# First block of the input projection: row scaling in halves ahead of all lo parts, and the hi products of three column groups in a row

## The chip, the cores and the metric

The kernel runs on one core of one Trainium2 chip. The metric is the device time of one execution in microseconds (us). Before the change the median of three runs was 921.94 us (920.85 to 922.54); the execution that was profiled took 920.29 us.

The engines are called PE (matrix products and transposes), DVE (vector work, two inputs), ACT (scalar work with one input: casts, copies, squares, activations), POOL (small scalar chains and some DMA issues) and SP (issues most DMAs). Each works its own list of instructions in order and waits on semaphores for the others.

## The reference, cut to what matters

There are 2048 prompt rows and 32 sample rows of width 1024. They run through one layer and a final norm:

```
hn   = rmsnorm(h, g_mix)                       # x * rsqrt(mean(x^2) + eps) * g
proj = hn @ w_in                               # 1024 -> 3072, six groups of 512 columns
hA, bA, cA, zA, vB, zB = split(proj)
u = cA * hA ;  c = causal width-3 conv(u) + bias ;  yA = bA * c * silu(zA)
yB = ((trailing mean(vB) - vB) @ pool_w) * pool_scale * silu(zB)
h += concat(yA, yB) @ w_out
h += (p @ w_ple) * sigmoid(rmsnorm(h, g_ple) @ w_gate)
y  = rmsnorm(h, g_final)
```

Everything is float32. A large product of two float32 operands is made of three PE products of rounded parts: each operand is split into a hi part (the value rounded to the PE's short float32 form) and a lo part (value minus hi), and hi*hi, hi*lo and lo*hi are added in PSUM.

## The kernel before

**Tiling.** The 2080 rows are cut into five blocks of 416 rows (`NB`). Blocks 0 and 1 form the first group. For the first of four column slices (`j = 0`), the first group is worked by `Unit.plain`: for each of the six column groups, 24 products of 128x128 weights by 128x416 rows per block, 8 pieces of the 1024 inner dimension by three part pairs. All later units use a scheme with seven products in place of eight; they are not touched.

**How the first block comes in.** SP loads rows 0 to 383 as three tiles of 128 rows, and then a fourth tile of 64 rows (the last 32 rows of block 0 and the last 32 of block 1). For each tile:

- ACT squares the row and adds it up (L89, `ssq_x`), POOL makes 1/root of it in two instructions (L70 `ms_x`, L74 `rstd_x`),
- DVE scales the tile by `rstd_x` and the gain (L407, `normal`),
- PE transposes it, four 128-column pieces to a PSUM bank, so two banks a tile: `pt_0_0` is the first half of tile 0, `pt_0_1` the second half (L416, `turn`),
- ACT writes the hi part with a cast (L78), DVE the lo part with a subtraction (L79), both from PSUM into the block's operand `B` (in `put`, by `split`).

The raw weights `raw_firstzb`, `raw_firstv` and `raw_firstc` of the first three column groups are split into hi and lo in the same way, as `w_firstzb`, `w_firstv` and `w_firstc`, two halves each.

**What PE does then.** `project` (L581) sorts the first product, `zb`, by part pair: 8 products hi*hi, 8 with the lo part of the rows, 8 with the lo part of the weights. All others (L564, `half_product`) take the three pairs for each piece in turn. After `zb` and `v` of block 0 come the transposes of block 1 (`pt_3`, `pt_0`, `pt_1`), the first half of `c`, the transposes `pt_2`, the second half of `c`, and then `zb` of block 1.

**Banks.** Six PSUM banks (`ps_m`) hold the transposes and products of this stage. A new tile takes the bank that came free longest ago in the program; the instruction that first writes it waits for the last reader of the old one. In the built program, the banks of `pt_0_0` and `pt_0_1` of block 0 go to its `pt_3_0` and `pt_3_1`, that of `pt_1_0` to `zb`, that of `pt_1_1` to `v`. In block 1, `pt_1_0` takes the bank of `zb` and `pt_1_1` that of `v`.

**What sets the order.** A scheduler orders each engine's instructions from the code; `keep_in_program_order` pins those it is called on to the order in which they are written. `second_block` is a generator whose steps (statistics, transposes, sums of block 1) are called between the products of block 0.

Of the kernel before, what the change touches and what calls it, by code (L numbers as in the profile page):

```python
# [12 lines left out]
ALU = mybir.AluOpType  # L13
PSUM = bass.MemoryType.PSUM

P = 128
D = 1024
KC = D // P
# [17 lines left out]
def trunk(ctx, tc, x_p, x_s, c_conv, c_pool, p_p, p_s, g_mix, w_in, conv_w, conv_b, pool_w,  # L36
# [294 lines left out]
    with ExitStack() as s1:  # L331
# [17 lines left out]
        def put(piece, src):  # L349

            return split(piece[:, :, 0], piece[:, :, 1], src)
# [52 lines left out]

        def normal(x, later=False):
            xt, n, r = x
            ins = nc.vector.scalar_tensor_tensor(xt[:n], xt[:n], r[:n], g_bc[:n], op0=ALU.mult, op1=ALU.mult)  # L407
            if later:
                tc.keep_in_program_order(ins)
# [156 lines left out]

        begun = []

        def project(ps, w, tb, between=None):
            x = hn[tb]  # L570
            if begun:
                for half in range(2):
                    half_product(ps, w[half], x[half], half == 0, half == 1)
                    if between and not half:
                        between()
                return

            begun.append(tb)
            steps = sorted(((k, a, b) for k in range(KC) for a, b in ((0, 0), (0, 1), (1, 0))), key=lambda t: t[1:])
            for i, (k, a, b) in enumerate(steps):  # L580
                nc.tensor.matmul(ps[:, :NB], w[k // KH][:, k % KH, a], x[k // KH][:, k % KH, b], start=i == 0,  # L581
                                 stop=i == len(steps) - 1)

# [9 lines left out]
        short0 = x_tile("0_3", [x_rows(0, 3), x_rows(1, 3)])  # L593
        B0.update(six(0))
        for c, x in enumerate([*ahead0, short0]):
# [84 lines left out]
        class Unit:  # L680
# [994 lines left out]
```

## Time and profile before

| | |
|---|---|
| median of three runs | 921.94 us |
| the profiled execution | 920.29 us |
| its span, first to last instruction | 918.5 us |
| PE busy | 904.2 us, 98% of the span |
| DVE busy | 722.4 us, 79% |
| ACT busy | 478.3 us, 52% |
| POOL busy | 150.8 us, 16% |

The span begins with the first instruction and ends with the last; the execution's own time is 1.8 us longer. Busy shares are means over the whole span. Where the order of a stage is in question, the list of instructions in order of time for that stage is the view to read, since shares do not tell which wait ended last.

### The profile page before, as it was taken

To read this page: it belongs to the slowest core of one execution; us is meant where nothing else is said; L and a number is where in the kernel's file an instruction comes from. 1 tells how busy PE (TensorE), PEld (TensorE's weight loads), DVE (VectorE), ACT (ScalarE), POOL (GpSimd) and SP (SyncE) were. 2 spreads that over 40 slices of the span, in tenths; PEclk is the share of its full clock that TensorE was granted. 3 is DMA by queue.
4 is the path that set the end of the run, shared out by engine and by line. 5 is a ranking of instruction groups with operands and counts; after the bars stand their busy time and mean duration, and the time that the engine had idled before them with its cause. 6 is when DMAs were issued, how large, how long until landed. Compare 5 with 4: busy or idle time off the path is not lost.

```text
span 918.5 us, 12937 instructions
## 1 busy us (share of the span) xinstructions
PE 904.2 (98%) x4485; PEld 819.3 (89%) x4485; DVE 722.4 (79%) x1231; ACT 478.3 (52%) x883; POOL 150.8 (16%) x271
## 2 busy tenths in 40 slices
PE   7999999999999999999999999999999999999996
PEld 5999999999999999999999988888877868888885
DVE  6996989999488989785777679765554799888965
ACT  6744565554345555443545456334334786565555
POOL 4111322212001111000000011111111002233333
PEclk9999999999999999999999999999999999999998
DMA  8245695779935546357655359755785886799893
GB/s 267 80 151 150 163 270 161 201 206 314 415 113 164 184 157 191 110 177 274 200 172 168 130 186 303 260 191 177 247 229 158 290 262 167 187 230 241 210 258 103
DMA packets 140734, 186.37 MB, mean 203 GB/s; under 512 B 12060, under 2 KB 111260, under 8 KB 139389
## 3 DMA queue, kind: packets, MB, share of 16 engines
q1 hardware_dynamic: 120237, 126.33, 45.0%
q0 software_dynamic: 17696, 53.71, 20.1%
q10 hardware_dynamic: 2736, 5.51, 1.8%
q8 instruction: 35, 0.57, 0.3%
q14 instruction: 30, 0.25, 0.1%
HBM read 128.93 MB, written 56.56 MB: 202 GB/s over the span
## 4 chain that ended last, share of the span: by engine, by line
PE 97%; DVE 1%; issue 1%; ACT 0%; DMA 0%; POOL 0%; SPq 0%; ACTq 0%; DVEq 0%; POOLq 0%
PE x_o L168 9%; PE x_g L168 9%; PE x_zbv L564 7%; PE x_ch L564 7%; PE x_zab L564 7%; PE e L103 5%; PE z_g L168 5%; PE z_o L168 4%; PE z_zbv L564 3%; PE z_ch L564 3%; PE z_zab L564 3%; PE v L564 3%; PE c L564 3%; PE b L564 3%; PE za L564 3%; PE h L564 3%
## 5 line engine op out<-in xcount | busy, mean ns | idle before, releaser
L78 ACT CAST y_S<-y_fS 128x512 fp32r<-128x512 f32 x32 | 19.3, 622 | 38.6 <-PE x_o L168 19.0
L103 PE MATMUL e<-wq,pps 128*128 128x512 f32 (+1 forms) x156 | 38.9, 400 | 0.2 <-ACT pps L78 0.2
L168 PE MATMUL x_o<-wo_b,y_S 128*128 128x512 f32 x128 | 35.8, 391 | 0.0
L168 PE MATMUL x_g<-wg_b,g_S 128*128 128x512 f32 x128 | 35.7, 389 | 0.0
L564 PE MATMUL z_zbv<-B,w_zbv_S 128*128 128x416 f32 x168 | 34.2, 352 | 0.0
L564 PE MATMUL x_ch<-B,w_ch_S 128*128 128x416 f32 x168 | 34.1, 351 | 0.0
L564 PE MATMUL z_zab<-B,w_zab_S 128*128 128x416 f32 x168 | 34.1, 351 | 0.0
L564 PE MATMUL x_zab<-B,w_zab_S 128*128 128x416 f32 x168 | 34.0, 351 | 0.0
L564 PE MATMUL x_zbv<-B,w_zbv_S 128*128 128x416 f32 x168 | 34.0, 351 | 0.0
L564 PE MATMUL z_ch<-B,w_ch_S 128*128 128x416 f32 x168 | 34.0, 351 | 0.0
L103 PEld LDWEIGHTS e<-wq,pps 128*128 128x128 f32 (+1 forms) x156 | 27.4, 182 | 7.0 <-ACT pps L78 0.5
L1402 POOL DMA_DIRECT2D e<-h_d x28 | 24.8, 906 | 52.9 <-DVE e L1399 45.9
L564 PEld LDWEIGHTS x_zab<-B,w_zab_S 128*128 128x128 f32 x168 | 31.3, 188 | 0.4
L564 PEld LDWEIGHTS x_zbv<-B,w_zbv_S 128*128 128x128 f32 x168 | 31.4, 188 | 0.3
L564 PEld LDWEIGHTS z_ch<-B,w_ch_S 128*128 128x128 f32 x168 | 31.4, 188 | 0.3
L564 PEld LDWEIGHTS z_zab<-B,w_zab_S 128*128 128x128 f32 x168 | 31.3, 188 | 0.3
L564 PEld LDWEIGHTS x_ch<-B,w_ch_S 128*128 128x128 f32 x168 | 31.3, 188 | 0.3
L564 PEld LDWEIGHTS z_zbv<-B,w_zbv_S 128*128 128x128 f32 x168 | 31.3, 188 | 0.4
L70 POOL TENSOR_SCALAR ms_x<-ssq_x 128x1 f32<-128x1 f32 (+2 forms) x18 | 11.0, 610 | 123.2 <-ACT junk L89 118.7
L78 ACT CAST y<-y 128x512 fp32r<-128x512 f32 x24 | 14.8, 618 | 29.2 <-PE x_o L168 14.6
L78 ACT CAST g_S<-g_fS 128x512 fp32r<-128x512 f32 x32 | 19.0, 618 | 18.5 <-DVE g_fS L1578 11.9
L168 PEld LDWEIGHTS x_o<-wo_b,y_S 128*128 128x128 f32 x128 | 24.0, 188 | 5.1 <-ACT c_o L1205 0.3
(598 smaller groups left out, 2651.5 us busy)
## 6 DMA issues: line engine op xcount, KB each, us to landing
y<-y_d SPq DMA_DIRECT2D x16, 512.0 KB, 5.6
x<-in_x_prompt_dram SPq DMA_DIRECT2D x16, 512.0 KB, 5.6
h_d<-x SPq DMA_DIRECT2D x16, 512.0 KB, 2.6
hn<-h_d SPq DMA_DIRECT2D x61, 128.0 KB, 6.2
xt<-in_x_prompt_dram SPq DMA_DIRECT2D x15, 512.0 KB, 5.4
e<-e_d SPq DMA_DIRECT2D x15, 512.0 KB, 6.4
e<-h_d POOLq DMA_DIRECT2D x28, 256.0 KB, 6.5
out_dram<-e POOLq DMA_DIRECT2D x13, 512.0 KB, 4.2
```

Of the source, the lines that this page charges most:

```text
L70: nc.gpsimd.tensor_scalar(ms[:n], ssq[:n], scalar1=1.0 / D, scalar2=EPS, op0=ALU.mult, op1=ALU.add)
L78: ins = nc.scalar.copy(hi, src)
L103: nc.tensor.matmul(ps[:n], pps[:, a, k, :n], wp[k][b][:, cs], start=k + q == 0, stop=k == 1 and q == 2)
L168: nc.tensor.matmul(ps[:n], lhs[:, k, a, :n], w[b][:, k], start=start and k + q == 0, stop=k == KH - 1 and q == 2, skip_group_check=True)
L564: nc.tensor.matmul(ps[:, :NB], lhs[:, k, x], b[:, k, y], start=start and k + q == 0, stop=stop and k == KH - 1 and q == 2, skip_group_chec ...
L1402: nc.gpsimd.dma_start(ee, h_d[r:r + P, at[1] * NH:at[1] * NH + NH], accum_op=ALU.add)
```

## The change

Three things are rewritten, all of them for block 0 of the first group at `j = 0`:

- `normal` takes a slice of columns. The four tiles of block 0 are scaled in eight steps of half a row each, all of them pinned, before the transposes are written. The lo parts, which stood between the scalings, come behind them.
- The hi casts of block 0 are pinned to the order in which they are written. The squares of the fourth tile come out ahead of all of them.
- `upper_parts` starts `zb`, `v` and `c` with their hi*hi products (8 each) in three banks, before anything else of these three is done. `lower_parts` adds the rest: 8 with the lo part of the rows, then 8 with the lo part of the weights. For `c` the rest is done half by half, with the transposes of block 1 between. Products of block 0 in these three groups are pinned.

The number of products, casts and subtractions and the numbers that they compute stay the same; only the four scalings become eight.

```
-        def normal(x, later=False):
+        def normal(x, later=False, cs=slice(0, D)):
             xt, n, r = x
-            ins = nc.vector.scalar_tensor_tensor(xt[:n], xt[:n], r[:n], g_bc[:n], op0=ALU.mult, op1=ALU.mult)
+            ins = nc.vector.scalar_tensor_tensor(xt[:n, cs], xt[:n, cs], r[:n], g_bc[:n, cs], op0=ALU.mult,
+                                                 op1=ALU.mult)
...
+        def part_of(ps, w, tb, half, a, b, start=False, stop=False):
+
+            x = hn[tb]
+            for k in range(KH):
+                tc.keep_in_program_order(
+                    nc.tensor.matmul(ps[:, :NB], w[half][:, k, a], x[half][:, k, b], start=start and k == 0,
+                                     stop=stop and k == KH - 1, skip_group_check=True))
+
+        def upper_parts(kind, w, tb):
+
+            ps = bank(f"{kind}_first")
+            for half in range(2):
+                part_of(ps, w, tb, half, 0, 0, start=half == 0)
+            begun[kind] = ps
+
+        def lower_parts(ps, w, tb, between):
+
+            order = [(half, *p) for p in ((0, 1), (1, 0)) for half in range(2)]
+            if between:
+                order.sort()
+            for i, (half, a, b) in enumerate(order):
+                part_of(ps, w, tb, half, a, b, stop=i == 3)
+                if between and i == 1:
+                    between()
...
+        for x in (*ahead0, short0):
+            for half in range(2):
+                normal(x, True, slice(half * NH, half * NH + NH))
         for c, x in enumerate([*ahead0, short0]):
-            normal(x)
             n = P if c < 3 else DEC
             for half, q in enumerate(("11", "21")):
-                put(B0[q][:, :, :, c * P:c * P + n], turn(x, half, f"pt0_{c}_{half}", bank)[:, :, :n])
+                ins = put(B0[q][:, :, :, c * P:c * P + n], turn(x, half, f"pt0_{c}_{half}", bank, True)[:, :, :n])
+                tc.keep_in_program_order(ins)
...
                 def product_of(kind, b, w, between=None):
+                    if kind in begun:
+                        ps = begun.pop(kind)
+                        lower_parts(ps, w, tbs[b], between)
+                        return ps[:, :NB]
...
                     wc = weights("c", j, f"c{tag}")
+                    for kind, w in (("zb", wz), ("v", wv), ("c", wc)):
+                        upper_parts(kind, w, tbs[0])
```

**DVE, the first block.** In the rows, `xt` is a tile of input rows, `B` the block's operand, `pt_a_b` half b of tile a transposed; the last numbers only tell buffers apart. Before:

```order
L407 SCALAR_TENSOR_TENSOR xt_0_162<-xt_0_162,rstd_x_0_168,g_bc 128x1024
L407 SCALAR_TENSOR_TENSOR xt_1_170<-xt_1_170,rstd_x_1_176,g_bc 128x1024
L407 SCALAR_TENSOR_TENSOR xt_2_178<-xt_2_178,rstd_x_2_184,g_bc 128x1024
L79 TENSOR_TENSOR B_0_195<-pt_0_0_199,B_0_195 128x4x128
L79 TENSOR_TENSOR B_0_195<-pt_0_1_206,B_0_195 128x4x128
L407 SCALAR_TENSOR_TENSOR xt_3_186<-xt_3_186,rstd_x_3_193,g_bc 64x1024
L79 TENSOR_TENSOR B_0_195<-pt_1_0_214,B_0_195 128x4x128
L79 TENSOR_TENSOR B_0_195<-pt_1_1_221,B_0_195 128x4x128
```

And now:

```order
L407 SCALAR_TENSOR_TENSOR xt_0_162<-xt_0_162,rstd_x_0_168,g_bc 128x512 x2
L407 SCALAR_TENSOR_TENSOR xt_1_170<-xt_1_170,rstd_x_1_176,g_bc 128x512 x2
L407 SCALAR_TENSOR_TENSOR xt_2_178<-xt_2_178,rstd_x_2_184,g_bc 128x512 x2
L407 SCALAR_TENSOR_TENSOR xt_3_186<-xt_3_186,rstd_x_3_193,g_bc 64x512 x2
L79 TENSOR_TENSOR B_0_195<-pt_0_0_206,B_0_195 128x4x128
L79 TENSOR_TENSOR B_0_195<-pt_0_1_213,B_0_195 128x4x128
L79 TENSOR_TENSOR B_0_195<-pt_1_0_220,B_0_195 128x4x128
L79 TENSOR_TENSOR B_0_195<-pt_1_1_227,B_0_195 128x4x128
L79 TENSOR_TENSOR B_0_195<-pt_2_0_234,B_0_195 128x4x128
```

The two lo parts of tile 0 (`pt_0_0`, `pt_0_1`) stood ahead of the fourth tile's scaling and stand behind it now.

**ACT, the same stage**, before:

```order
L89 ACTIVATE raw_firstc,ssq_x_2_180<-xt_2_178 128x1024
L78 CAST B_0_195<-pt_0_0_199 128x4x128
L78 CAST B_0_195<-pt_0_1_206 128x4x128
L89 ACTIVATE junk,ssq_x_3_189<-xt_3_186 64x1024
L78 CAST B_0_195<-pt_1_0_214 128x4x128
L78 CAST B_0_195<-pt_1_1_221 128x4x128
L78 CAST B_0_195<-pt_2_0_229 128x4x128
L78 CAST B_0_195<-pt_2_1_236 128x4x128
L78 CAST w_firstzb_259<-raw_firstzb 128x4x128
L78 CAST B_0_195<-pt_3_0_244 128x4x32
L78 CAST B_0_195<-pt_3_1_251 128x4x32
L78 CAST w_firstzb_262<-raw_firstzb 128x4x128
```

And now:

```order
L89 ACTIVATE raw_firstc,ssq_x_2_180<-xt_2_178 128x1024
L89 ACTIVATE junk,ssq_x_3_189<-xt_3_186 64x1024
L78 CAST B_0_195<-pt_0_0_206 128x4x128
L78 CAST B_0_195<-pt_0_1_213 128x4x128
L78 CAST B_0_195<-pt_1_0_220 128x4x128
L78 CAST B_0_195<-pt_1_1_227 128x4x128
L78 CAST B_0_195<-pt_2_0_234 128x4x128
L78 CAST B_0_195<-pt_2_1_241 128x4x128
L78 CAST B_0_195<-pt_3_0_248 128x4x32
L78 CAST w_firstzb_263<-raw_firstzb 128x4x128
L78 CAST B_0_195<-pt_3_1_255 128x4x32
L78 CAST w_firstzb_266<-raw_firstzb 128x4x128
```

The fourth tile's squares moved ahead of the hi casts. The first weight cast (`w_firstzb`, first half) stood ahead of the cast of `pt_3_0` and stands behind it now.

**PE, the first products**, before:

```order
L416 MATMUL pt_3_0_244<-ident,xt_3_186 128x64 x4
L416 MATMUL pt_3_1_251<-ident,xt_3_186 128x64 x4
L581 MATMUL zb_0_0_325<-B_0_195,w_firstzb_259 128x416 x4
L581 MATMUL zb_0_0_325<-B_0_195,w_firstzb_262 128x416 x4
L564 MATMUL v_0_0_351<-B_0_195,w_firstv_266 128x416
L581 MATMUL zb_0_0_325<-B_0_195,w_firstzb_259 128x416 x4
L581 MATMUL zb_0_0_325<-B_0_195,w_firstzb_262 128x416 x4
L581 MATMUL zb_0_0_325<-B_0_195,w_firstzb_259 128x416 x4
L581 MATMUL zb_0_0_325<-B_0_195,w_firstzb_262 128x416 x4
L564 MATMUL v_0_0_351<-B_0_195,w_firstv_266 128x416 x11
L564 MATMUL v_0_0_351<-B_0_195,w_firstv_269 128x416 x12
```

And now:

```order
L417 MATMUL pt_3_1_255<-ident,xt_3_186 128x64 x4
L582 MATMUL zb_first<-B_0_195,w_firstzb_263 128x416 x4
L582 MATMUL zb_first<-B_0_195,w_firstzb_266 128x416 x4
L582 MATMUL v_first<-B_0_195,w_firstv_270 128x416 x4
L582 MATMUL v_first<-B_0_195,w_firstv_273 128x416 x4
L582 MATMUL c_first<-B_0_195,w_firstc_279 128x416 x4
L582 MATMUL c_first<-B_0_195,w_firstc_282 128x416 x4
L582 MATMUL zb_first<-B_0_195,w_firstzb_263 128x416 x4
L582 MATMUL zb_first<-B_0_195,w_firstzb_266 128x416 x4
L582 MATMUL zb_first<-B_0_195,w_firstzb_263 128x416 x4
L582 MATMUL zb_first<-B_0_195,w_firstzb_266 128x416 x4
L582 MATMUL v_first<-B_0_195,w_firstv_270 128x416 x4
```

All hi*hi products of `zb`, `v` and `c` stand first now, so 8 products of `c` are ahead of the rest of `zb` and `v`. In the built program the three started products hold three of the six banks at once, and the banks are handed out anew behind them: in block 1, `pt_1_0` takes the bank of `v`, and `pt_1_1` that of block 1's `pt_3_0`, whose last reader is ACT's copy of it into `xt_3`.

**ACT, behind the copy of `v`** (`V`), where block 1's transposes are read, before:

```order
L798 COPY V_0_321<-v_0_0_351 128x416
L78 CAST B_12_285<-pt_3_0_386 128x4x32
L78 CAST B_2_197<-pt_3_1_394 128x4x32
L78 CAST pw<-raw_pw 128x512
L78 CAST B_12_285<-pt_0_0_402 128x4x128
L627 COPY xt_3_186<-pt_3_0_386 128x128
```

And now:

```order
L823 COPY V_0_325<-v_first 128x416
L78 CAST B_12_289<-pt_3_0_399 128x4x32
L78 CAST B_2_197<-pt_3_1_407 128x4x32
L78 CAST B_12_289<-pt_0_0_415 128x4x128
L78 CAST B_2_197<-pt_0_1_423 128x4x128
L648 COPY xt_3_186<-pt_3_0_399 128x128
```

The cast of `pw` went ahead of the copy of `V`, and the cast of `pt_0_1` came ahead of the copy of `pt_3_0` into `xt_3`.

More of the change, by code (lines that the diff above doesn't have):

```diff
@@ L565, in half_product @@
                                      stop=stop and k == KH - 1 and q == 2, skip_group_check=True)
-        begun = []
+        begun = {}
         def project(ps, w, tb, between=None):
             x = hn[tb]
[L571 to L582, printed above, removed]
+            for half in range(2):
+                half_product(ps, w[half], x[half], half == 0, half == 1)
+                if between and not half:
+                    between()
[17 more added lines that the diff above has]
+                if between and i == 1:
+                    between()
         B0 = {}
@@ L594, in trunk @@
         B0.update(six(0))
+        for x in (*ahead0, short0):
+            for half in range(2):
+                normal(x, True, slice(half * NH, half * NH + NH))
         for c, x in enumerate([*ahead0, short0]):
-            normal(x)
             n = P if c < 3 else DEC
             for half, q in enumerate(("11", "21")):
-                put(B0[q][:, :, :, c * P:c * P + n], turn(x, half, f"pt0_{c}_{half}", bank)[:, :, :n])
+                ins = put(B0[q][:, :, :, c * P:c * P + n], turn(x, half, f"pt0_{c}_{half}", bank, True)[:, :, :n])
+                tc.keep_in_program_order(ins)
         hn[0] = B0["11"], B0["21"]
```

## The prediction

> **What bounds the kernel now.** I read the page of the profile first: busy shares, and the chain of work that ended last.
>
> ```profile
> span 918.5 us, 12937 instructions
> PE 904.2 (98%) x4485; PEld 819.3 (89%) x4485; DVE 722.4 (79%) x1231; ACT 478.3 (52%) x883; POOL 150.8 (16%) x271
> PE 97%; DVE 1%; issue 1%; ACT 0%; DMA 0%; POOL 0%; SPq 0%; ACTq 0%; DVEq 0%; POOLq 0%
> ```
>
> PE carries 97% of the chain. Next, the view of waits for PE (who was waited for, us in total, times, longest):
>
> ```profile
> PE gm L376 <- DMA gm_row<-in_g_mix_dram: 2.4, 1, 2.4
> PE pt L416 <- DVE xt L407: 2.3, 1, 2.3
> PE pt L416 <- issue: 1.3, 1, 1.3
> PE x_zab L564 <- DVE U L880: 0.3, 1, 0.3
> PE e L103 <- ACT pps L78: 0.2, 1, 0.2
> ```
>
> The first three lie in the first 15 us; behind them PE waits 0.5 us in 900. So whatever delays PE in the first 35 us stays in the time almost whole, and there is little for the change to win behind its own place. Third, PE's instructions in order of time (start, length, name, count):
>
> ```profile
> 8.44 4.87 PE L416 MATMUL pt<-ident,xt 128*128 128x128 f32 x24 [2.29 <-DVE xt L407]
> 14.61 0.68 PE L416 MATMUL pt<-ident,xt 64*128 64x64 f32 x8 [1.29 <-issue]
> 15.39 2.88 PE L581 MATMUL zb<-B,w_firstzb 128*128 128x416 f32 x8
> 18.07 0.55 PE L564 MATMUL v<-B,w_firstv 128*128 128x416 f32 x1
> 18.41 3.51 PE L581 MATMUL zb<-B,w_firstzb 128*128 128x416 f32 x16
> 21.77 4.50 PE L564 MATMUL v<-B,w_firstv 128*128 128x416 f32 x23
> 26.20 2.60 PE L416 MATMUL pt<-ident,xt 64*128 64x64 f32 x24
> 34.17 2.06 PE L564 MATMUL zb<-B,w_firstzb 128*128 128x416 f32 x10
> ```
>
> From 15.39 on every row begins where the one before lets it. The first nine products take (18.41 - 15.39)/9 = 0.34 us each, the 23 of `v` (26.20 - 21.77)/23 = 0.193. The view by windows tells why (length, PE busy, number, granted clock, DMA):
>
> ```profile
> 12.36:15.77 3.41, 2.01 (x18) 0.99 1.11 346
> 15.77:19.18 3.41, 3.41 (x12) 0.51 0.71 248
> 19.18:22.59 3.41, 3.41 (x20) 1.00 0.78 221
> ```
>
> In one stretch of 3.41 us the clock was half, behind a stretch in which PE was busy for 2.01 of 3.41 us.
>
> **Part 1: when the first product can start.** Here DVE, POOL and ACT set the time. DVE:
>
> ```profile
> 7.10 1.28 DVE L407 SCALAR_TENSOR_TENSOR xt<-xt,rstd_x,g_bc 128x1024 f32<-128x1024 f32 x1 [0.22 <-ACT raw_firstv L89]
> ...
> 10.83 1.28 DVE L407 SCALAR_TENSOR_TENSOR xt<-xt,rstd_x,g_bc 128x1024 f32<-128x1024 f32 x1 [0.72 <-POOL rstd_x L74]
> 12.04 1.28 DVE L79 TENSOR_TENSOR B<-pt,B 128x512 fp32r<-128x512 f32 x2
> 13.24 1.27 DVE L407 SCALAR_TENSOR_TENSOR xt<-xt,rstd_x,g_bc 64x1024 f32<-64x1024 f32 x1
> 14.43 2.86 DVE L79 TENSOR_TENSOR B<-pt,B 128x512 fp32r<-128x512 f32 x6
> 19.62 1.28 DVE L79 TENSOR_TENSOR w_firstc<-raw_firstc,w_firstc 128x512 fp32r<-128x512 f32 x2
> ```
>
> POOL (`ms_x` of tile 1, `rstd_x` of tiles 2 and 3, then block 1):
>
> ```profile
> 7.12 0.19 POOL L70 TENSOR_SCALAR ms_x<-ssq_x 128x1 f32<-128x1 f32 x1 [0.42 <-ACT raw_firstv L89]
> ...
> 10.25 0.55 POOL L74 TENSOR_TENSOR rstd_x<-ms_x,nhalf 128x1 f32<-128x1 f32 x1
> 12.43 0.54 POOL L74 TENSOR_TENSOR rstd_x<-ms_x,nhalf 64x1 f32<-64x1 f32 x1
> 19.32 1.63 POOL L70 TENSOR_SCALAR ms_x<-ssq_x 128x1 f32<-128x1 f32 x1 [6.35 <-ACT junk L89]
> 21.04 0.55 POOL L74 TENSOR_TENSOR rstd_x<-ms_x,nhalf 128x1 f32<-128x1 f32 x1
> 21.67 1.28 POOL L70 TENSOR_SCALAR ms_x<-ssq_x 128x1 f32<-128x1 f32 x1
> ```
>
> ACT:
>
> ```profile
> 9.08 0.19 ACT L89 ACTIVATION_READ_ACCUMULATOR raw_firstc<-xt 128x1 f32 x1
> 13.88 0.63 ACT L78 CAST w_firstzb<-raw_firstzb 128x512 fp32r<-128x512 f32 x1
> 15.07 0.52 ACT L78 CAST B<-pt 128x128 fp32r<-128x128 f32 x2 [0.56 <-PE pt L416]
> ```
>
> Before: the fourth scaling ends at 13.24 + 1.27 = 14.51, its transposes start at 14.61, their cast at 15.07, and the product at 15.39 as soon as the first of the two casts is done. `w_firstzb` had been cast at 13.88, in ACT's idle time.
>
> Now the squares of the fourth tile follow those of the third at 9.27 and end near 10.4 instead of 12.1. That gain is mostly lost on POOL. Its 0.2 us step `ms_x` took 1.63 us at 19.32 and ended at 20.95, just behind DVE's row that ends at 19.62 + 1.28 = 20.90: while DVE runs such rows back to back, POOL stands still, at the borders between them too. The row at 21.67, 0.05 us behind the start of a scaling, is the same again. So `ms_x` of tile 3 finds POOL free at 10.80, comes 0.05 us behind the third tile's scaling at 10.83, and gets through at its end: 10.83 + 1.28 + 0.05 = 12.16; 0.08 to the next as from 20.95 to 21.04, then 0.55 of `rstd_x`: 12.79. The scaling in two halves I take at 1.28 as the whole one was; if each half costs as a 512-wide row of 0.68, less the overlap of 0.08, it is the same. It ends at 14.07, 0.44 earlier than before.
>
> But the lo parts now stand behind it, and the transposes need the banks that these free: one row each 0.60 us, ends at 14.67, 15.27 and 15.87. `pt_3_0` starts at 14.72, `pt_3_1` at 15.33 (before: 14.61, and the last four right behind), and `zb` needs the third lo part's bank: 15.93. On ACT, the cast of `pt_3_0` runs from 15.17 and the cast of the first weights, now behind it, from 15.34 for 0.63: 15.97. Both ends agree: the first product starts at 16.0, **0.6 us later**. The nearest rows bound this: if POOL slips through ahead of the third scaling (as its row at 7.12 did, 0.02 us behind a start), all of it is 0.68 earlier and the start is the old one; if the weight cast waited for both small casts, it would be 0.2 more.
>
> What the later start costs depends on the clock: in the half-clock stretch a product takes 0.34 instead of 0.193, so a later start of 0.6 loses 0.6/0.34 = 1.8 products, worth 0.35 us at full speed, and a little more as the clock was still full up to 15.77. I take **+0.4**; with another position of the stretch it is up to +0.6.
>
> **Part 2: the products.** Their number is the same. 8 products of `c` (8 x 0.193 = 1.54 us) move ahead of the rest of `zb` and `v`. `zb` and `v` end 1.54 us later and `c` is shorter by the same behind them: nothing by itself. Its cover is the time between the end of `v` and block 1's `zb`, which falls from 34.17 - 26.20 = 7.97 to 6.43 us. What has to be done in it is on ACT and DVE:
>
> ```profile
> 26.30 0.51 ACT L798 COPY V<-v 128x416 f32<-128x416 f32 x1 [2.79 <-PE v L564]
> 26.71 0.50 ACT L78 CAST B<-pt 128x128 fp32r<-128x128 f32 x2
> 27.11 0.62 ACT L78 CAST pw<-raw_pw 128x512 fp32r<-128x512 f32 x1
> 27.62 0.59 ACT L78 CAST B<-pt 128x512 fp32r<-128x512 f32 x1
> 28.10 0.28 ACT L627 COPY xt<-pt 128x128 f32<-128x128 f32 x1
> 32.95 0.69 DVE L79 TENSOR_TENSOR B<-pt,B 128x512 fp32r<-128x512 f32 x1
> ```
>
> The last row is the lo part of `pt_2_0`, which block 1's `zb` needs with its second product: 33.64 against 34.36, a slack of 0.7. In the changed order the lo part of `pw` and that of `f` (0.60 us a row each) are no longer ahead of it, so it comes 7.44 - 1.2 = 6.2 us behind the end of `v`, against a need at 6.43 + 0.19 = 6.6: it still fits.
>
> **Part 3: a new wait.** `pt_1_1` of block 1 now writes the bank that ACT's copy of `pt_3_0` frees. Counted from the start of the transposes (26.20 before): the cast of `pt_0_0` can start when its four transposes are done, some 1.3 behind (8 small ones and 4 at 0.11, 0.27 for the last one's end, 0.1 at the start); at 27.62 it came at 1.42 with the cast of `pw` ahead. Then the cast of `pt_0_1` at 0.48 behind, then the copy, again 0.48 behind, for 0.28: it ends at 1.33 + 0.48 + 0.48 + 0.28 = 2.57. `pt_1_1` was issued 20 transposes behind the start, at 2.0. PE waits to 2.63: **+0.63**. Behind this wait stand on PE the rest of `c` and all that follows; DVE and ACT gain time by it, so the lo part above fits all the more. The ends: nothing, if the cast of `pt_0_1` were not in the way (-0.48) and the rows ran at their shortest; 0.8, if each of the four rows takes 0.04 more, as the cast of 0.63 at 13.88 did against that of 0.59.
>
> **What is hidden.** `zb`'s activation and the copy of `V` come 1.5 us later; the next reader on PE is the pooling product behind `v` of block 1, over 15 us on. The raw weights of `h`, `za` and `b` wait on SP for lo parts that end about 0.9 later; before, the last of these ends at 20.90, over 13 us ahead of block 1's `zb`, and the products of `h` stand behind that. POOL's and ACT's later order is the old one but for neighbours that change places.
>
> **The sum**: +0.4 + 0.63 = +1.05 us. Made against the profiled execution it gives 920.29 + 1.05 = 921.3; that execution lies 1.65 below the median, about what one half-clock stretch more or less is worth. Set on the median: 921.94 + 1.05 = **923.0 us**. What this measurement can tell from no change is about 0.2%, 1.84 us.
>
> **The rivals.**
>
> *A second half-clock stretch (slower).* The wait of 0.63 leaves a window of 3.41 us busy for at most 82%, and before the first product three gaps (1.4, 0.2 and 0.3 us) take the place of one of 1.3. The rows show only that 59% busy was followed by half clock, and 100% by full; 82% lies in the middle. Where it decides against the kernel, a stretch costs 3.41 x (1 - 0.193/0.34) = 1.5 us whole, less where it meets a stretch that was slow before: +1.9 to +2.6, some 924.2. The Trainium skill, in "TensorE: Matmul & The Clock Gate", Part 1, says that half clock comes back only after at least one idle window, and that windows run freely of the kernel's start. By that rule there would be no such stretch at all, and no slow one at 15.77 either: the sum would be +0.6 + 0.63 = 1.23. The trace here differs, as the window ahead of 15.77 was not idle.
>
> *A further wait on ACT or DVE in block 1 (slower).* By part 2 the lo part of `pt_2_0` comes 0.4 ahead of its need, so from a delay of 0.4 on it would hold PE. One or two more waits of the size of part 3's would make +1.7 to +2.3, some 924.0. Against it: PE's own wait gives both engines 0.63.
>
> *The start is not later (same).* If POOL gets through as at 7.12, part 1 is nought: +0.6, 922.5.
>
> *Faster.* Transposes that start earlier (each half row is released alone) could fill a window so that the clock stays full at the first products: 11 products at 0.193 instead of 0.34, -1.6. With both waits it ends at -0.4, and only without a later start too is it near -1.0: 920.9.
>
> **How the numbers follow.** Both waits and no further stretch: 0.45, between +0.6 and +1.6. A further stretch: 0.36. A further wait: 0.09. Start not later: 0.07. Faster: 0.03. The first and fourth lie within 0.2%: 0.52. The second and third lie over it: 0.45. The last counts as faster by over 0.2% only with the scatter of the runs shown, 0.9 us each way: 0.03. The likeliest case alone gives 922.5 to 923.5; the range takes in the second case at its upper end and the scatter below: 921.4 to 924.7.
>
> **What would show it.** In the changed kernel's rows: the fourth scaling's end near 14.1 and the first product near 16.0 (an earlier product shows part 1 wrong); PE waiting about 0.6 us at a transpose near 30 us for ACT's copy of `xt` (no such wait shows part 3 wrong); the granted clock in windows of 3.41 us up to 35 us; no new wait of PE behind block 1's `zb`. A PE wait there for a lo part, or a second window at half clock, would make the forecast too low.

## The result

| | median | runs |
|---|---|---|
| before | 920.87 us | 19 |
| after | 922.9 us | 19 |

The ratio after to before is 1.0022 (95% interval 1.0015 to 1.0029): the change costs 2.0 us (1.4 to 2.7). The forecast of 923.0 us is met to 0.1, but not for its reasons alone. It was set on a median of 921.94 for the kernel before, from three runs; in the runs beside the changed kernel that median is 920.87. So the base was 1.1 us too high, and the cost, forecast as 1.05 us, 1.0 too low. The two errors cancelled.

The profiled execution of the changed kernel took 922.48 us. From its page, the span and the busy times:

```profile
span 920.7 us, 12945 instructions
PE 905.9 (98%) x4485; PEld 820.0 (89%) x4485; DVE 723.5 (79%) x1235; ACT 478.1 (52%) x883; POOL 152.3 (17%) x271
```

From its view of waits for PE (us in total, times, longest):

```profile
PE pt L417 <- DVE xt L407: 1.4, 1, 1.4
PE pt L417 <- DVE B L79: 1.1, 1, 1.1
PE pt L417 <- ACT xt L648: 0.5, 1, 0.5
PE x_o L168 <- DVE c_o L1227: 0.4, 1, 0.4
...
PE zb_first L582 <- ACT w_firstzb L78: 0.3, 1, 0.3
```

PE waits for a lo part where the gap of 1.3 us before the change was put down to nothing that shows ("issue"), then for the weight cast, and then for ACT's copy. The same waits in PE's order of time:

```profile
14.51 1.06 PE L417 MATMUL pt<-ident,xt 64*128 64x64 f32 x8 [1.14 <-DVE B L79]
15.84 2.17 PE L582 MATMUL zb_first<-B,w_firstzb 128*128 128x416 f32 x8 [0.28 <-ACT w_firstzb L78]
...
30.77 0.66 PE L417 MATMUL pt<-ident,xt 128*128 128x128 f32 x4 [0.46 <-ACT xt L648]
...
35.27 0.92 PE L565 MATMUL zb<-B,w_firstzb 128*128 128x416 f32 x4
```

The first product comes at 15.84 instead of 15.39, PE stands idle for 0.46 at `pt_1_1`, and `zb` of block 1 starts at 35.27 instead of 34.17: 1.10 later. The idle time is not the whole delay: the 24 transposes ahead of `c` now take 3.29 us (28.14 to 31.43) instead of 2.60, 0.69 more, since PE also loses the overlap of one transpose with the next. The other 0.4 is the later start.

The two profiled executions differ by 2.19 us, twice as much. Of the rest, by the times at which PE comes to the same instructions, 0.26 is lost near 107 us and 0.7 near 569 us; the section on e5 comes back to these. DVE ahead of the first product, in order of time; each row is now a pair of halves:

```profile
8.73 1.42 DVE L407 SCALAR_TENSOR_TENSOR xt<-xt,rstd_x,g_bc 128x512 f32<-128x512 f32 x2 [0.45 <-POOL rstd_x L74]
10.59 1.41 DVE L407 SCALAR_TENSOR_TENSOR xt<-xt,rstd_x,g_bc 128x512 f32<-128x512 f32 x2 [0.44 <-POOL rstd_x L74]
12.44 1.41 DVE L407 SCALAR_TENSOR_TENSOR xt<-xt,rstd_x,g_bc 64x512 f32<-64x512 f32 x2 [0.44 <-POOL rstd_x L74]
```

POOL in the same time, the step `ms_x` of tiles 2 and 3:

```profile
8.78 0.75 POOL L70 TENSOR_SCALAR ms_x<-ssq_x 128x1 f32<-128x1 f32 x1
...
10.64 0.75 POOL L70 TENSOR_SCALAR ms_x<-ssq_x 64x1 f32<-64x1 f32 x1
```

The fourth scaling ends at 13.85, 0.66 earlier than before, and yet the first product is 0.45 later. One profile of each kernel does not fix these two times: in a second profile of the kernel before (e5) the scaling ends at 14.82 and the first product comes at 15.89. What holds in both is the distance between them, 0.88 and 1.07 before the change and 1.99 behind it. The windows (length, PE busy, number, granted clock, DMA share, GB/s):

```profile
13.62:17.03 3.41, 2.11 (x14) 1.00 1.07 367
17.03:20.44 3.41, 3.41 (x12) 0.50 0.34 102
...
27.27:30.68 3.41, 3.04 (x26) 1.00 0.42 120
30.68:34.09 3.41, 3.32 (x23) 1.00 0.13 39
```

One window at half clock, as before. The two windows that hold the wait of 0.46 are followed by full clock.

### The profile page after: what moved, and what is told of

Same layout as the page of the kernel before. It is cut to its first block, busy times and chain, and to the rows that moved or that the text cites. A ratio compares the mean times of both kernels' runs of the same rounds, so it can differ in the third digit from the quotient of the medians.

```text
span 920.7 us, 12945 instructions
## 1 busy us (share of the span) xinstructions
PE 905.9 (98%) x4485; PEld 820.0 (89%) x4485; DVE 723.5 (79%) x1235; ACT 478.1 (52%) x883; POOL 152.3 (17%) x271
## 4 chain that ended last, share of the span: by engine, by line
PE 92%; DMA 3%; DVE 2%; ACT 1%; POOL 1%; issue 1%; SPq 0%; ACTq 0%; DVEq 0%; POOLq 0%
PE x_g L168 9%; PE x_o L168 8%; PE x_zab L565 7%; PE x_zbv L565 7%; PE x_ch L565 6%; PE e L103 5%; PE z_g L168 5%; PE z_o L168 4%; PE z_zbv L565 3%; PE z_zab L565 3%; PE b L565 3%; PE z_ch L565 3%; PE za L565 3%; PE h L565 3%; PE v L565 2%; PE c L565 2%
## 5 line engine op out<-in xcount | busy, mean ns | idle before, releaser
L1227 DVE TENSOR_TENSOR c_o<-x_o,x 128x512 f32<-128x512 f32 x14 | 9.7, 691 | 23.9 <-PE x_o L168 23.9
```

Of the source, the lines that this page charges most:

```text
L1227: add = lambda o, a, b: nc.vector.tensor_tensor(o, a, b, op=ALU.add)
```

## The experiments

All are timed against the kernel before on the same chip. `e1` to `e4` ran together, then `e5` to `e8`, `e9` to `e11`, and `e12`. "Gap filled" stands for ten idle transposes ahead of `pt_3_0`. The columns from the profiles are the end of the fourth scaling, the start of the first product, PE's idle time at `pt_1_1` for ACT's copy, how much longer block 1's transposes take than in the kernel before (2.60 us for the first 24, 1.04 for the 8 of `pt_2`), and the start of block 1's `zb`. A wait that is mostly covered by the overlap of two transposes shows no idle time in the rows, but it shows in the fourth of these columns.

| | ratio to before (95%) | scaling 4 ends | first product | idle at `pt_1_1` | transposes longer by | `zb`, block 1 |
|---|---|---|---|---|---|---|
| before | 1 | 14.51 | 15.39 | none | 0 | 34.17 |
| after | 1.0022 (1.0015, 1.0029) | 13.85 | 15.84 | 0.46 | 0.69 | 35.27 |
| e1 products alone | 1.0001 (0.9992, 1.0010) | 14.76 | 15.80 | none | 0.29 | 34.45 |
| e2 scaling alone | 1.0011 (1.0002, 1.0020) | 14.59 | 16.80 | none | 0 | 36.77 |
| e3 other bank | 1.0012 (1.0004, 1.0021) | 13.96 | 15.95 | none | 0.36 (`pt_2`) | 36.09 |
| e4 after, again | 1.0019 (1.0006, 1.0031) | 13.86 | 15.85 | 0.46 | 0.69 | 35.08 |
| e5 before, again | 1.0001 (0.9993, 1.0010) | 14.82 | 15.89 | none | 0 | 34.28 |
| e6 before, gap filled | 1.0011 (1.0000, 1.0021) | 14.70 | 16.39 | none | 0 | 33.67 |
| e7 after, gap filled | 1.0009 (0.9998, 1.0020) | 14.15 | 16.18 | 0.87 | 1.10 | 34.51 |
| e8 weight cast first | 1.0013 (1.0004, 1.0022) | 14.21 | 16.15 | none | 0.20 | 36.13 |
| e9 lo parts first | 1.0003 (0.9994, 1.0011) | 14.68 | 15.43 | none | 0.20 | 34.38 |
| e10 e9, gap filled | 1.0004 (0.9994, 1.0014) | 15.20 | 15.94 | 0.99 | 1.21 | 34.36 |
| e11 whole rows | 1.0021 (1.0012, 1.0030) | 14.43 | 16.53 | 0.46 | 0.69 | 36.99 |
| e12 e10, other bank | 0.9993 (0.9984, 1.0003) | 15.34 | 16.82 | none | 0.19 (`pt_2`) | 34.11 |

### The two parts apart (e1, e2)

e1 sets the scaling part of the change back, and with it the pins on the casts:

```
-        for x in (*ahead0, short0):
-            for half in range(2):
-                normal(x, True, slice(half * NH, half * NH + NH))
         for c, x in enumerate([*ahead0, short0]):
+            normal(x)
...
-                ins = put(..., turn(x, half, f"pt0_{c}_{half}", bank, True)[:, :, :n])
-                tc.keep_in_program_order(ins)
+                put(..., turn(x, half, f"pt0_{c}_{half}", bank)[:, :, :n])
```

> Only the products are changed (hi parts of zb, v and c first, three banks held); scalings, squares and lo parts stand as before. Theory A (two waits: a later first product, and a wait of block 1's transposes for ACT's copy of xt): the first product starts as before, near 15.4 us, and only the second wait is there, some 0.5 us; the time is 0.5 to 0.9 us over before. Theory B (the clock: longer or more stretches at half clock cost most of the 2.0 us): no gap ahead of the first product is added, so it stays within 0.5 us of before. Rival C (the cost lies far behind, in waits of PE for DVE at 570 and 760 us): the time is 1.5 us or more over before, with such waits in the list of PE's waits.

e2 is the reverse: the kernel before, with these lines and the slice in `normal` put in.

> Only the scaling is changed (halves, ahead of the lo parts, casts pinned, squares of the fourth tile first); the products stand as before. Theory A: the first product starts 0.4 to 0.5 us later, near 15.85, behind the first weight cast, there is no wait for a copy of xt in block 1's transposes, and the time is 0.3 to 0.6 us over before. Theory B: the gaps ahead of the first product are here too, so most of the 2.0 us is here: 1.2 to 1.8 us over before. Rival C: 0.3 to 0.6 us, and no waits at 570 us.

The products alone cost nothing measurable (0.1 us, -0.7 to 0.9). That is less than theory A's 0.5 to 0.9, though the interval still reaches it. The scaling alone costs 1.0 us (0.2 to 1.8). The wait for ACT's copy is in e1 too, but short. Its 24 transposes:

```profile
27.71 2.89 PE L417 MATMUL pt<-ident,xt 64*128 64x64 f32 x24
```

That is 0.29 more than the 2.60 before. With the new products, `pt_1_1` takes the bank that this copy frees; in e1 ACT's copy of `pt_3_0` still runs ahead of the cast of `pt_0_1`, and only with the cast ahead of it does the delay grow to 0.69. e2 has none of it. In e2's profile the third tile's load came late (ACT waited 1.9 us for it), and with it the third and fourth scaling; and the full clock was first granted at 22.80. Both make its first product and `zb` late, so its time is read from the ratio, not from that profile.

### The bank of `pt_1_1`, and the change once more (e3, e4)

e3 lets the two transposes of `pt_3` in block 1 write the two banks that `pv` and `pm` use, and puts `pv` behind the first products of `c`:

```
-                    pt = turn(x, half, f"pt1_{c}_{half}", bank, later=True)[:, :, ts]
+                    pt = turn(x, half, f"pt1_{c}_{half}", tbank if c == 3 else bank, later=True)[:, :, ts]
...
-                            vectors()
                             c_block(b, lambda: next(second))
+                            vectors()
```

> The changed kernel, with block 1's two short transposes in the two other PSUM banks and the transpose of the vectors behind c, so that none of block 1's transposes waits for ACT's copy of xt. Theory A: the wait of 0.46 us goes and the first product stays near 15.8; the time is 0.4 to 0.5 us under the changed kernel's. Theory B: it gains that and, with one gap less, a little more, 0.5 to 1.0 us. If the lo part of pt_2_0 becomes the next limit, less than 0.3 us is gained and PE waits for DVE's B ahead of block 1's zb.

e4 is the changed kernel, unaltered.

> The changed kernel once more, for a second profile beside the kernel before on the same chip. Theory A and B: 1.5 to 2.5 us over before; 1.1 us of it by block 1's zb in the profile. The waits of PE for DVE at 106, 570 and 760 us: if they belong to the change they are there again at the same size (0.28, 0.68, 0.2 us); if they are the scatter of one execution they are elsewhere or gone.

In e3 no wait for ACT's copy is left among PE's waits:

```profile
PE pt L417 <- DVE xt L407: 2.2, 2, 1.9
PE pt L417 <- DVE B L79: 1.3, 1, 1.3
PE x_zab L565 <- DVE U L907: 0.3, 1, 0.3
```

But it has moved, to `pt_2_1`, and is shorter. The 8 transposes of `pt_2` take 0.36 more than the 1.04 before:

```profile
33.31 1.40 PE L417 MATMUL pt<-ident,xt 128*128 128x128 f32 x8
```

`zb` is late mainly for another reason: two windows at half clock stand one behind the other.

```profile
11.58:14.99 3.41, 1.88 (x14) 1.00 1.13 337
14.99:18.40 3.41, 3.22 (x13) 0.50 0.93 337
18.40:21.82 3.42, 3.42 (x11) 0.50 0.68 193
```

e4 gives the 0.46 again. Over all kernels with the changed order of the lo parts and no filled gap, those whose transposes take 0.69 more stand at 1.0022, 1.0019 and 1.0021, those with 0 to 0.36 (e2, e3, e8) at 1.0011, 1.0012 and 1.0013. The difference of the means, 0.0009, is 0.8 us. It is rough: each ratio is uncertain by 0.6 to 1.2 us, and the kernels differ in other things too.

### Do the later waits belong to the change? (e5)

The changed kernel's profile has two more small waits far behind, at `x_ch` (0.2 idle, near 107 us) and at `x_o` (0.4, near 569 us), and e4 had them too. They are the 0.26 and the 0.7 of the result.

> The kernel before, unchanged, profiled once more. In three profiles that hold the new order of the products (the changed kernel twice, and the products alone) PE waits 0.3 to 0.4 us for DVE's row that writes c_o near 569 us, because a load of y lands 14.4 to 14.8 us behind its issue; in the three others (before, the scaling alone, the other bank) the load takes 13.8 to 13.9 and there is no such wait. If the wait belongs to the new order, this profile shows none of more than 0.1 us near 569 us, and a load under 14.0; if the landing simply scatters, such a profile of the kernel before can show the wait too. The time is the old one either way, within 0.5 us.

The kernel before shows the wait at `x_o` in its second profile:

```profile
570.03 0.50 PE L168 MATMUL x_o<-wo_a,y_S 128*128 128x512 f32 x1 [0.31 <-DVE c_o L1200]
```

In that profile a load of `y` landed 15.3 us behind its issue, against 13.9 in the first. So this wait follows the landing of loads, which scatters, and is not the change's: over all fourteen profiles it came in the four in which the load took 14.4 us or more, and in none of the others. It costs this second profile 0.7 us, and the profile is 1.40 us longer than the first, though the kernel is the same. `x_ch` waited 0.5 in e6, also without the change, but both profiles of the changed kernel have it and both of the kernel before do not; that the change has no part in this 0.26 is not shown.

### The clock (e6, e7)

Ten transposes whose result nobody reads fill the gap ahead of `pt_3_0`, in the kernel before (e6) and in the changed one (e7):

```
+            if c == 3:
+                kept = tbank("kept")
+                for _ in range(10):
+                    tc.keep_in_program_order(nc.tensor.transpose(kept[:, :P], ident, ident))
```

> The kernel before with 10 transposes of ident (no use is made of them, about 0.11 us each) between the transposes of pt_2_1 and pt_3_0, in a gap of 1.3 us in which PE stood still. Theory: the half clock of 3.41 us at the first products follows from the idle share of the window ahead (59% busy). With the gap filled there is no half clock up to 35 us, the block 1 zb comes at 32.7 instead of 34.2 and the time falls by about 1.5 us, 0.3 less where two neighbours on ACT change places. Rival: the half clock comes at that time of the kernel whatever stands ahead of it; then the time is the old one, at most 0.3 us more.

> The changed kernel with the same 10 transposes in its gap of 1.14 us ahead of pt_3_0. Theory of the clock: no half clock ahead of block 1's zb, which comes at 33.8 instead of 35.3, and a time 1.5 us under the changed kernel's. Were the half clock what makes the changed kernel slower than before, the two kernels with the filled gap would differ by less than those without: under 0.5 us; if it is the later first product and the wait for the bank, they differ by more than with half clock, since a later start of 0.45 us then costs all of it: 0.45 + 0.46 = 0.9 us or more. Rival (half clock whatever stands ahead): as the changed kernel.

The clock did as the theory said. e7's windows:

```profile
10.45:13.86 3.41, 3.25 (x16) 1.00 1.12 336
13.86:17.27 3.41, 3.00 (x24) 1.00 1.08 370
17.27:20.69 3.42, 3.42 (x20) 1.00 0.36 105
```

The time followed only in part. e7 stands at 1.0009, about 1.1 us under the changed kernel (1.0022 and 1.0019), where 1.5 was expected, and the intervals overlap. e6 stands at 1.0011, over the kernel before, where 1.5 us less was expected. In e6 the full clock was granted from 14.66 on, so the ten transposes ran slower, 1.51 us in all, and pushed the first product to 16.39; `zb` still came 0.5 earlier. In its profile PE then loses 0.6 near 107 us, and 3.8 by a wait near 848 us and the half clock behind it; what e6's other runs lost where is not known. In e7 PE came to `pt_1_1` earlier than ACT's copy could, and the wait grew:

```profile
30.02 0.66 PE L417 MATMUL pt<-ident,xt 128*128 128x128 f32 x4 [0.87 <-ACT xt L652]
```

So 0.76 of the 1.5 us that a window at half clock costs came back (`zb` at 34.51 instead of 35.27). The rest went into a later start (16.18 instead of 15.84, as the fourth scaling ended at 14.15) and into the longer wait (0.87 idle instead of 0.46). The Trainium skill, in "TensorE: Matmul & The Clock Gate", Part 1, has half clock come back after at least one idle window. The rows here differ: in all nine profiles that have it, it follows a window that PE filled to between 1.51 and 2.11 of 3.41 us (44 to 62%), and in the first 40 us no window at full clock that PE filled to 2.43 us or more was followed by it. e6 shows the same far behind, where a wait of 1.9 us at `x_g` leaves a window of 1.51 and the next one is at half clock (these two rows list PE, PE's weight loads, DVE, ACT and POOL, then the clock):

```profile
847.50:850.93 3.43, 1.51 (x8) 0.92 (x7) 3.39 (x5) 1.29 (x3) 0.74 (x2) 1.00 0.93 210
850.93:854.34 3.41, 3.41 (x10) 2.64 (x9) 3.26 (x4) 0.62 (x2) 1.47 (x2) 0.50 0.79 148
```

The busy share alone is not the rule, though. At the end of the span, where PE has run out of work, windows of 1.70 us (the changed kernel), 1.77 (e9) and 1.91 (e11), 50 to 56% busy, were still followed by full clock, and windows of 0.83 (before), 0.92 (e3) and 1.12 (e12) by half. What else counts is open.

### What makes the first product late (e8, e9)

e8 moves ACT's cast, by splitting `zb`'s weights before the fourth tile is transposed. On DVE the lo parts of these weights go ahead of those of the fourth tile, from 17.73 on, behind the first product:

```
         for c, x in enumerate([*ahead0, short0]):
             n = P if c < 3 else DEC
+            if c == 3:
+                made.append(weights("zb", 0, "firstzb"))
```

> The changed kernel with the weights of zb split ahead of the fourth tile's transposes, so that ACT's cast of the first weights runs in its idle time near 14 us, as before the change, and not behind the cast of pt_3_0; the lo parts of these weights go ahead of those of the fourth tile on DVE. Part 1 as forecast has two ends that agree, the banks and the cast. By it the first product then waits for the bank alone that the third lo part frees, and starts at 15.5 to 15.6 instead of 15.84, and not at 15.4 as in the kernel before. If the cast alone made it late, it starts right behind the last transposes, at 15.4. If the banks alone did, it stays at 15.8. ACT's copy of pt_3_0 stands one cast earlier in its queue, so the wait at pt_1_1 should shrink from 0.46 to 0.1 or nothing. Time: 0.3 to 0.7 us under the changed kernel.

This missed by 0.6 us: the first product came at 16.15. Part of that is a fourth scaling that ended 0.36 later (14.21 instead of 13.85). Measured from its end, 1.65 to 1.75 was expected and 1.94 came, hardly less than in the changed kernel (1.99). The lo parts begin at 14.13 and take 0.60 each, so the third one ends near 16.0, and the product follows it.

```profile
14.87 1.29 PE L417 MATMUL pt<-ident,xt 64*128 64x64 f32 x8 [1.79 <-DVE B L79]
```

The cast does not set it; with the cast out of the way, the banks hold PE for nearly as long.

e9 sets one thing back, on DVE: the two lo parts of tile 0 go ahead of the fourth scaling.

```
-        for x in (*ahead0, short0):
+        for x in ahead0:
             for half in range(2):
                 normal(x, True, slice(half * NH, half * NH + NH))
...
                 tc.keep_in_program_order(ins)
+            if c == 0:
+                for half in range(2):
+                    normal(short0, True, slice(half * NH, half * NH + NH))
```

> The changed kernel with one thing set back: on DVE the two lo parts of the first tile stand ahead of the fourth scaling again, as in the kernel before. ACT's cast of the first weights goes ahead of the cast of pt_3_0 by itself, and the copy of pt_3_0 one place earlier. So far the first product comes 1.9 to 2.0 us behind the end of the fourth scaling in every kernel with the changed scaling whose clock was full at the transposes (13.85 to 15.84, 13.87 to 15.85, 13.96 to 15.95, 14.16 to 16.18, 14.21 to 16.15), and 0.88 behind it in the kernel before (14.51 to 15.39). Theory (the lo parts behind the fourth scaling make the first product late): here it comes 0.8 to 1.0 behind the fourth scaling, which ends at 14.5 to 14.8, so at 15.4 to 15.7; the wait at pt_1_1 falls from 0.46 to at most 0.15; the time is that of the kernel before within 0.7 us (under 921.8), against +2.0 for the change as it is. Rival (the halves, the pinned order or the products cost the time by themselves): the time stays 1.2 us or more above the kernel before.

DVE in e9, where the scaling of 64 rows stands behind two lo parts:

```profile
12.08 1.28 DVE L79 TENSOR_TENSOR B<-pt,B 128x512 fp32r<-128x512 f32 x2
13.28 1.40 DVE L407 SCALAR_TENSOR_TENSOR xt<-xt,rstd_x,g_bc 64x512 f32<-64x512 f32 x2
```

And PE in e9:

```profile
15.43 2.56 PE L582 MATMUL zb_first<-B,w_firstzb 128*128 128x416 f32 x8 [0.17 <-ACT w_firstzb L78]
34.38 1.86 PE L565 MATMUL zb<-B,w_firstzb 128*128 128x416 f32 x9
```

The scaling ends 0.83 later than in the changed kernel, and the first product comes 0.41 earlier: 0.75 behind the scaling, not 1.99. No idle time is left at `pt_1_1`, and the transposes take 0.20 more than before instead of 0.69, as the copy of `pt_3_0` stands one place earlier on ACT. The time is that of the kernel before (1.0003). Halves, pins and the new order of the products are all still in it; so the place of two lo parts, with the two places on ACT that came with it, is the cost.

### Filling the gap without the late lo parts (e10, e12)

e10 is e9 with the ten transposes; e12 is e10 with e3's banks.

> The kernel of the run above with the 10 transposes of ident ahead of pt_3_0. In ten profiles up to now a window of 3.41 us at full clock that PE filled to 1.51 to 2.11 us was followed by one at half clock (7 of 7), and one that it filled to 2.54 us or more was not (all). With the gap filled no half clock is expected at the first products; block 1's zb at 33.3 to 33.9 and a time 0.5 to 1.0 us under the run above, so at or a little under the kernel before. If the clock does not matter to the time, it is the same as the run above.

> The kernel with the lo parts first and the 10 transposes, and in it the two transposes of pt_3 in block 1 write the two tiles that pv and pm use, so that pt_1_1 needs no bank that ACT has yet to free; pv goes behind the products of c. With full clock at the first products PE came to pt_1_1 earlier and waited 0.99 there for ACT's copy (0.46 at half clock). If the wait ate what the clock gave, block 1's zb now comes about 1.0 earlier, at 33.2 to 33.6 against 34.2 in the kernel before, and the time is 0.5 to 1.0 us under the kernel before. If ACT and DVE are the bound there as well, the wait comes back at the next place, at zb of block 1 for a lo part or at pt_2_0 for a bank, and zb stays at 34.0 or later; then the time is that of the kernel before.

e10 had full clock at the first products and a wait of 0.99 in exchange, so its time stayed (1.0004 against 1.0003), where 0.5 to 1.0 us less was expected:

```profile
29.85 0.66 PE L417 MATMUL pt<-ident,xt 128*128 128x128 f32 x4 [0.99 <-ACT xt L655]
```

e12 has only 0.19 of it, at `pt_2_1`, and its median is the lowest of all, 920.79 us against 921.28 for the kernel before beside it. But the interval (0.9984 to 1.0003) still includes 1, no change, and `zb` came at 34.11 instead of 33.2 to 33.6. Its profile was no fair test of the 1.0 us: the third tile's scaling began at 11.41, late behind its load, and the full clock came only at 15.69.

### Halves or whole rows (e11)

```
         for x in (*ahead0, short0):
-            for half in range(2):
-                normal(x, True, slice(half * NH, half * NH + NH))
+            normal(x, True)
```

> The changed kernel with each of its scalings as one row of 1024 instead of two of 512; their place in the order stays. In every profile of the halves a pair took 1.41 us, and a step of POOL got in between the halves (0.75 at 8.78 in the changed kernel). If POOL gets in only at the border of two rows of DVE, then with whole rows its step ms_x of a tile that comes while a scaling runs ends with that scaling, 1.2 us or more behind its own start, as in the kernel before; the scalings take 1.28 and stand 0.6 to 0.7 apart instead of 0.44, and the fourth ends at 13.9 to 14.3, not earlier than with halves: the halves buy nothing, since what they gain on POOL they lose on DVE. If the halves were cheaper, it would end at 14.4 or later. The wait for the bank stays at 0.4 to 0.6, and the time within 0.7 us of the changed kernel's.

DVE with whole rows, the third and the fourth scaling:

```profile
11.16 1.28 DVE L407 SCALAR_TENSOR_TENSOR xt<-xt,rstd_x,g_bc 128x1024 f32<-128x1024 f32 x1 [0.72 <-POOL rstd_x L74]
13.15 1.28 DVE L407 SCALAR_TENSOR_TENSOR xt<-xt,rstd_x,g_bc 64x1024 f32<-64x1024 f32 x1 [0.71 <-POOL rstd_x L74]
```

POOL in the same kernel:

```profile
9.28 1.22 POOL L70 TENSOR_SCALAR ms_x<-ssq_x 128x1 f32<-128x1 f32 x1 [0.15 <-ACT raw_firstc L89]
...
11.21 1.28 POOL L70 TENSOR_SCALAR ms_x<-ssq_x 64x1 f32<-64x1 f32 x1
```

With whole rows POOL's step lasts until the scaling's end (1.28), with halves until the first half's (0.75). Scalings then follow one another by 1.99 to 2.00 us, with halves by 1.85 to 1.86, though a pair takes 1.41. From the start of the first scaling the fourth ends 7.27 behind with whole rows (7.16 to 14.43), 6.97 with halves (6.88 to 13.85). So the halves do help, by 0.3 us, against the first theory here; in this order the help ends at the banks, and the times of the two kernels do not differ (1.0021 and 1.0022). The Trainium skill, in "SBUF — State Buffer", section "SBUF: two separate sides", says that a DVE instruction with two inputs in SBUF, as the scaling has, and a POOL instruction that reads SBUF take a shared pair of ports in turn, for a whole instruction each. These rows agree. The step of 1.63 us at 19.32 in the kernel before, which lasts across a border between two DVE rows, is not explained by it.

e11 had two windows at half clock again:

```profile
11.86:15.28 3.42, 1.66 (x14) 1.00 1.11 342
15.28:18.69 3.41, 3.23 (x14) 0.50 0.77 285
18.69:22.10 3.41, 3.41 (x11) 0.50 0.53 151
```

## Why the prediction was right, and where it was not

**The sum** names two terms, and in the profiles both are right. The delay at `pt_1_1` was forecast at +0.63 and took 0.69; the later start was forecast at +0.4 and took the other 0.41 of the 1.10 by block 1's `zb` (0.22 in e4; against the second profile of the kernel before, 0.30 and 0.11). Together at most 1.10, against 1.05. What failed is the step from there to the time: as far as the clocks below show, it left out what a second window at half clock adds in part of the runs. The measured cost is 2.0 us (1.4 to 2.7), and only the base, 1.1 too high, brought forecast and time together. That is luck.

**The fourth scaling.** Forecast 14.07, measured 13.85, and the whole difference is that the first scaling began 0.22 earlier (6.88 instead of 7.10); counted from there both are 6.97. Two steps failed on the way and cancelled: a pair of halves takes 1.41, not 1.28, and POOL does get in between two halves, which the prediction denied from the row at 19.32. That row spanned the border of two lo parts; between halves of a scaling POOL got through, and the next scaling began 1.85 behind the one before instead of 1.96.

**The first product.** Forecast 16.0 from two ends that agree, the banks and the weight cast; measured 15.84, and 15.85 in e4. From the end of the fourth scaling the forecast had 1.93, and 1.99 came. The banks are shown to be enough for it: e8 takes away the cast and PE still starts 1.94 behind the scaling; e9 takes away both and it is 0.75. That the cast would be enough alone no run shows; in the changed kernel PE waited for it last, 0.28.

**What the later start costs** was forecast as +0.4, with the half-clock window taking up part of the delay. By `zb` that is about what came in the profiles with one such window. But kernels with this order whose transposes are held up by 0 to 0.36 (e2, e3, e8) stand 1.0 to 1.2 us above before. In the profiles of e3, e8 and e11 a second window at half clock followed the first, worth up to 1.5 us. In these three PE filled the first half-clock window to 3.22, 3.39 and 3.23 us; in the five where it was full (3.41), full clock followed, and in e4 it followed on 3.19. So a gap ahead of the first products, when it falls into that window, seems to be able to keep the clock down.

The runs without a profile bear on this too, as each has its mean granted clock on record. It counts half clock wherever it stood, the end of the span included. It leaves out what lies ahead of the first full clock (e2's profile has 0.998). Profiles with one window at half clock near the start have 0.995 to 0.997, those with two 0.993 to 0.995, so 0.995 can be either. A mean of 0.995 or less came in 11 of 116 runs of the kernel before, in 14 of 30 of the changed kernel (with e4), in 22 of 34 of e2, e3 and e8, and in none of 46 with the gap filled. So the changed kernel does lose the clock more often. Its 16 other runs took 922.7 us on average, 1.3 above the like runs of the kernel before (921.4, on several chips), and the 14 took 924.0. An estimate from these means: 1.3 of the cost (0.5 either way) is there with the clock alike, which fits the 1.05 of the sum, and some 0.6 comes from the runs with more half clock. One thing does not fit: e9 has a mean of 0.995 or less in 5 of 11 runs, with the old order of the lo parts, and yet the time of the kernel before. Where these runs lose the clock, and why it costs them less, is open.

**The wait at `pt_1_1`.** The forecast has `pt_1_1` start 2.63 behind the first transpose of block 1; it started 2.63 behind (28.14 to 30.77), in e4 as well. Cause and place are as forecast. The 0.46 that the list of waits shows is less than the delay of 0.69; the idle time grows to 0.87 and 0.99 when PE is faster ahead of it.

**The products at nothing.** Right: e1 is 1.0001, and no lo part of block 1 held PE in any profile.

**The rivals.** The second half-clock window, given 0.36, is the rival that came: in the profiles of e3, e8 and e11, and by the mean clocks in part of the changed kernel's runs. Of its two places, the wait near 30 us was none: its windows (3.04 and 3.32 us busy, and 2.95 in e4) were followed by full clock. It came behind the first window, where the gaps ahead of the first product lie. The further wait in block 1 did not come. Start not later, and faster: no.

**The three classes.** 0.22% (0.15 to 0.29) lies on the border that the prediction drew at 0.2%, so neither "same" nor "slower" is refuted.

## What to carry to other kernels

Before a row is moved ahead on an engine, count what now stands behind it that frees a buffer: two subtractions that nobody waited for by name held two PSUM banks, and cost more than the earlier scaling gained. Measure a delay by when the work behind it starts, not by the idle time alone: 0.46 idle was 0.69 lost. And price a gap on PE with the window that it falls into: a gap of 1.1 to 1.3 us brought 3.41 us at half clock with it, while filling the gap gained little as long as the next engine in the chain could not follow.

## What was not expected of the hardware

- Near the start, half clock returned after windows that PE filled to 44 to 62%, never after one of 71% or more; at the end of the span it did not return right behind windows of 50 to 56%.
- Two halves of a scaling cost 1.41 us on DVE against 1.28 for the whole, and still shorten a chain that goes through POOL by 0.14 a tile (1.85 instead of 1.99 from one scaling to the next).
- Two profiles of the same kernel before differ by 1.40 us, half of it at one wait for a load. The same load of `y` landed between 13.5 and 15.3 us behind its issue in different profiles; PE's wait of 0.3 to 0.4 near 569 us comes and goes with it. Waits of up to 2.1 us near 850 us came in two profiles (e6, e10); their cause was not followed.
